# Padded pools with 64-byte shifts, a new order inside attention items, and bias tiles on the GpSimd queue in a two-layer diffusion backbone

## The chip, the cores and the metric

The kernel runs on one core of one Trainium2 chip. A core has TensorE (PE in the profile; its weight loads are PEld), VectorE (DVE), ScalarE (ACT), GpSimd (POOL) and SyncE (SP), one on-chip memory (SBUF) of 128 partitions, and matmul accumulators (PSUM). Transfers between main memory and SBUF are requested on the queues of SP, POOL and ACT. The metric is the device time of one execution in microseconds.

## The reference

The reference computes two layers over 1,024 latent tokens (`x`, on a grid of 16 rows by 64 columns) and 256 context tokens, each of width 1,024:

- layer 0: RMS norm and modulation, an input projection (1,024 to 2,048 columns), a 2-D Fourier transform over 512 of the channels beside an order-2 Hyena long convolution over the others, and an output projection; then a SwiGLU feed-forward network (FFN) with 2,816 hidden units, for latent and context tokens.
- layer 1: neighbourhood attention with 16 heads of 64, then output projection and FFN for the latent tokens alone, and a last RMS norm.

In the attention a latent query sees a window of local keys with a bias per relative position, and all context keys, in one softmax:

```python
s_loc = einsum(q_r, k_b) * scale + bias          # masked outside the window
s_ctx = einsum(q_r, kc) * scale
p = softmax(concatenate([s_loc, s_ctx], axis=-1), axis=-1)
o = einsum(p_loc, v_b) + einsum(p_ctx, vc)
```

## The kernel before

**Number format and matmuls.** Weights and activations of nearly all products are split in two fp32r parts, high and low (`split`, lines 278 to 282: ACT copies the high part, DVE subtracts to get the low one), and three matmuls (high·high, high·low, low·high) take the place of one. Each matmul loads its stationary operand anew. Widths of the moving operand are 512 for latent tokens (`pc` 0 and 1), 256 for context tokens (`pc` 2) and 384 for the local keys in attention.

**Pools.** SBUF is cut into tile pools in the order of their creation (lines 205 to 211): `cp` (constants), `p4` (20 tiles of 4 KB per partition), `p2` (35 of 2 KB), `pg` (4 of 2 KB), `pt` (6 of 2 KB and small ones), `pko` (4 of 2 KB, named `tk`), `pw` (two each of `wh`, `wl`, `ws`, 4 KB). Tiles of `p4` and `p2` are named `s` in the profile, of `pg` `g`, of `pt` `t`; `mat` and `cs` are other names for the slots of `pw`. In the built program every tile of `p4`, `p2`, `pg` and the 2 KB tiles of `pt` starts 96 bytes past a multiple of 128 bytes, and every tile of `pko` and `pw` 32 bytes past one.

**Who uses `pw`.** `weights` (line 292) loads 512 KB of a weight matrix into `ws` or an `s` tile and splits it to a pair from `pair2` (`wh` and `wl`) or, in the context FFN, `pair3` (every third pair from the two `ws` slots). The high and low parts are then stationary operands of `lin` (line 319), whose moving operands are `s` tiles: input projection (16 blocks of 128 columns, each 8 row blocks, 3 matmuls, widths 256, 512 and 512), output projection (8 blocks, widths 512 and 256, and then 512 alone), context FFN (22 blocks for gate and up, width 256), the key and query projections in `attn_prep`, and the second output projection. Queries and the second output projection read the moving operand through a strided view with runs of 16 numbers (64 bytes). In `values` the roles are turned: `wh` and `wl` are the moving operand. `cmat` (line 306) loads a Fourier matrix as fp16 into `ws` and ACT widens it to `mat`, which is stationary in the spectra (width 512) and moving in the inverse transform `hy_inverse` (width 256). The latent FFN is a Strassen-Winograd scheme with seven products (`wino_steps`, matmuls at line 1246); two of the seven take their weights from `wh` and `wl`, the others from `s` and `t` tiles. Its down projection (`down`, line 1413) has both operands in `s` tiles; the context's down projection (line 1516) takes weights from `wh` and `wl` at width 256.

**Order.** A scheduler orders the instructions of each engine from its own estimate of times; buffers that come free and the order in which the program text creates the work set the rest. Each engine and each queue works in order.

**Attention.** `attention` (line 1648) runs 64 items (head, half of the rows, pair of column groups) through three stages, one item ahead, and weaves in the projections of the next pair of heads (`attn_prep`), or at the end the first part of the output projection (`first_part`), as other work for PE. Stage 1 of `attn_item` (line 1674) requests two bias tiles (`g`, 192 KB each, on SP's queue, `pg` has four) and computes context scores of both groups into one PSUM tile and local scores into two. Stage 2: DVE takes the maximum of the context scores (L1699), adds the bias and takes the maximum for each group (L1701), negates both maxima in one instruction (L1703); ACT makes four exponentials in the order bias tile 0, context 0, bias tile 1, context 1 (L1706, L1707); DVE adds the sums and inverts them (L1709, L1710); PE transposes the context probabilities and then each group's local ones (L1715), ACT and DVE split them into two fp16 parts (L1718, L1719). Stage 3 multiplies by the values, 30 matmuls of 64 columns. On POOL's queue in this stretch are copies of the halves of the queries into the other 64 partitions (`s<-s`, line 1632), stores of the attention's output (`d<-tk`, from L1757 and L1758), and, near the end, pieces of the output projection's weights (`ws<-in_w_out`) and the residual stream.

Of the kernel before, what the change touches and what calls it, by code (L numbers as in the profile page):

```python
# [10 lines left out]
F32 = mybir.dt.float32  # L11
F32R = mybir.dt.float32r
F16 = mybir.dt.float16
AF = mybir.ActivationFunctionType
# [4 lines left out]
P = 128  # L19
# [11 lines left out]
KSTART = (0, 8, 24, 32)  # L31
BOPS = ("B11", "B21", "T2", "T1", "T3", "B22", "T4")
# [167 lines left out]
class Builder:  # L200
    def __init__(self, ctx, tc, a, out, taps=None, stop=None):
        self.tc, self.nc, self.a, self.out = tc, tc.nc, a, out
        self.taps, self.stop = taps, stop
        ent = ctx.enter_context
        self.cp = ent(tc.tile_pool(name="cp", bufs=1))
        self.p4 = ent(tc.tile_pool(name="p4", bufs=20))
        self.p2 = ent(tc.tile_pool(name="p2", bufs=35))
        self.pg = ent(tc.tile_pool(name="pg", bufs=4))
        self.pt = ent(tc.tile_pool(name="pt", bufs=6))
        self.pko = ent(tc.tile_pool(name="pk", bufs=4))  # L210
        self.pw = ent(tc.tile_pool(name="pw", bufs=2))
        self.pp = ent(tc.tile_pool(name="pp", bufs=6, space=bass.MemoryType.PSUM))
        self.pq = ent(tc.tile_pool(name="pq", bufs=2, space=bass.MemoryType.PSUM))
        self.dr = ent(tc.tile_pool(name="dr", bufs=1, space=bass.MemoryType.DRAM))
        self.k = self.mk = self.pk = 0
        self.banks = 8
        self.sq = {}

# [67 lines left out]

    def pair3(self):

        self.p3 = (getattr(self, "p3", 0) + 1) % 3
        return self.pair2(("ws", "ws") if self.p3 == 0 else ("wh", "wl"))  # L290

    def weights(self, src, w=1024, cut=False, keep=None, wide=False, load=None):
        st = self.S4() if wide else self.pw.tile([P, 1024], F32, tag="ws", name=self.nm("ws"))
        if keep:
            hi, lo = keep
        else:
            hi, lo = self.pair3() if wide == 3 else self.pair2()
        (load or self.ld)(st.rearrange("p (n k) -> p n k", n=4) if cut else st[:, :w], src)
        self.split(st[:, :w], hi[:, :w], lo[:, :w])
        return hi, lo  # L300
# [5 lines left out]
    def cmat(self, w, src, view=None, small=False):  # L306
# [8 lines left out]
        m = self.mat(w)  # L315
# [506 lines left out]
    def hy_inverse(self, sq, o, y):  # L822
# [8 lines left out]
        for h in range(H // hw):  # L831
# [25 lines left out]
            for part, fi, i, fb in mats:  # L857
                ms[(i, fb)] = self.cmat(min(nb, 2) * 512, a["vi_" + sq][h, i, :, fb:fb + min(nb, 2)],
                                        lambda t: t.rearrange("p (f c) -> p f c", c=512), False)
# [431 lines left out]
    def ffn(self, l, u, h, hs, second, after, keep=None, begun={}):  # L1291
# [21 lines left out]
        todo = iter(())  # L1313
        if u is not None:
            for fb in range(NFB):
                wide = 3 if fb < NFB - 2 else True
# [77 lines left out]
    def down(self, l, bops, sops, hidc, hs, h, todo, after, keep):  # L1394
# [98 lines left out]
        if l == 0:  # L1493
# [4 lines left out]
            for kb in range(NFB):  # L1498
# [9 lines left out]
                wh, wl = self.pair2()  # L1508
# [165 lines left out]
    def attn_item(self, head, hd, hf, c0, qs, kk, kc, vt, osb, out):  # L1674
# [5 lines left out]
        for i in (0, 1):  # L1680
            c = c0 + i
            b = self.G(F32, 384)
            self.ld(b, a["bias"][head, hf, c])
# [15 lines left out]
        nc.vector.tensor_reduce(cm, pctx.rearrange("p (i k) -> p i k", i=2), axis=AX, op=MAX)  # L1699
        for i in (0, 1):  # L1700
            nc.vector.tensor_tensor_reduce(bias[i], loc[i][:, :384], bias[i], 1.0, cm[:, i:i + 1], ADD, MAX,  # L1701
                                           mx[:, i:i + 1])
        nc.vector.tensor_scalar(nm, mx, -1.0, None, op0=MUL)  # L1703
        pc = self.T()
        for i in (0, 1):
            nc.scalar.activation(bias[i], bias[i], AF.Exp, bias=nm[:, i:i + 1], accum_out=s1[:, i:i + 1])  # L1706
            nc.scalar.activation(pc[:, i * 256:i * 256 + 256], pctx[:, i * 256:i * 256 + 256], AF.Exp,  # L1707
                                 bias=nm[:, i:i + 1], accum_out=s2[:, i:i + 1])
        nc.vector.tensor_tensor(s1, s1, s2, ADD)  # L1709
        nc.vector.reciprocal(rv, s1)  # L1710
        pts = []
        for src, n in ((pc, 4), (bias[0], 3), (bias[1], 3)):
# [7 lines left out]
            pts.append(t)  # L1720
# [437 lines left out]
```

## Time and profile before

| | |
|---|---|
| median of three runs | 3058.11 us (3051.83 to 3061.61) |
| the profiled execution | 3055.81 us, span 3054.0 us |
| granted TensorE clock, mean | 0.985 |
| matmuls | 16,320 |
| ACT busy, POOL busy (share of span) | 46%, 15% |
| moved by DMA | 549.87 MB, mean 180 GB/s |
| largest group of matmuls | L1246, `s` by `s`, 2,028 of 128x512 |

In the profile a row such as `ps<-s,wh` names the output tile, the moving operand and the stationary operand, with buffer numbers left out. Times are microseconds from the start of the span. A matmul's shown duration reaches into the next one's, since they are pipelined; the distance between starts is what one costs.

### The profile page before, as it was taken

How to read it: one execution, taken by the hardware profiler on the slowest of the kernel's cores; microseconds unless marked ns; L12 is line 12 of the kernel's file. 1: busy time of each engine (PE TensorE's matmuls, PEld its weight loads, DVE VectorE, ACT ScalarE, POOL GpSimd, SP SyncE). 2: the span in 40 equal slices, each digit the busy share in tenths (PEclk: the TensorE clock that was granted, in tenths of full speed). 3: DMA queues.
4: the chain of work that ended last, by engine and by line, in shares of the span. 5: the costliest groups of instructions: out<-in, count | busy, mean ns of one | idle time of the engine just before them, and what ended most of it. 6: DMA issues, size and time to landing. Idle time of an engine off the chain costs nothing. (4 is left out here: it accounts for less than half of the span.)

```text
span 3054.0 us, 45753 instructions
## 1 busy us (share of the span) xinstructions
PE 2919.6 (96%) x16320; PEld 2420.3 (79%) x16320; DVE 2076.6 (68%) x3924; ACT 1390.4 (46%) x2581; POOL 460.3 (15%) x751
## 2 busy tenths in 40 slices
PE   7899999999999999999999999999889999999997
PEld 2678888888899788787778888888777788887886
DVE  5767785775677777866677437777676977664545
ACT  4663225453454333333445336777675533333433
POOL 1012012451101111212010000110111022112000
PEclk9999999999999999999999999999999999999999
DMA  6564545466555454659874334454555266535663
GB/s 250 190 204 169 182 141 155 124 199 206 210 172 200 170 181 170 215 177 325 299 252 165 131 126 116 127 143 124 164 180 187 97 234 221 173 111 175 214 193 131
DMA packets 263486, 549.87 MB, mean 180 GB/s; under 512 B 33878, under 2 KB 85784, under 8 KB 263258
## 3 DMA queue, kind: packets, MB, share of 16 engines
q1 hardware_dynamic: 209658, 381.23, 38.5%
q0 software_dynamic: 51296, 161.52, 15.1%
q10 hardware_dynamic: 2304, 4.20, 0.4%
q8 instruction: 128, 2.10, 0.3%
q14 instruction: 100, 0.82, 0.1%
HBM read 418.63 MB, written 119.80 MB: 176 GB/s over the span
## 5 line engine op out<-in xcount | busy, mean ns | idle before, releaser
L1246 PE MATMUL ps<-s,s 128*128 128x512 f32 x2028 | 513.0, 395 | 14.3 <-ACT g L1251 11.0
L1246 PEld LDWEIGHTS ps<-s,s 128*128 128x128 f32 x2028 | 384.6, 190 | 103.4 <-ACT g L1251 13.4
L276 PE MATMUL ps<-s,wh 128*128 128x256 f32 (+1 forms) x1768 | 391.7, 327 | 1.3 <-ACT wh L280 1.3
L276 PEld LDWEIGHTS ps<-s,wh 128*128 128x128 f32 x1768 | 291.4, 188 | 37.2 <-ACT wh L280 3.4
L276 PE MATMUL pq<-s,wh 128*128 128x512 f32 (+1 forms) x984 | 300.9, 384 | 10.3 <-DVE s L1630 7.6
L280 ACT CAST wh<-ws 128x1024 fp32r<-128x1024 f32 (+1 forms) x139 | 142.6, 1026 | 351.2 <-PE ps L276 163.2
L1413 PE MATMUL ps<-s,s 128*128 128x512 f32 (+1 forms) x1000 | 258.6, 384 | 11.2 <-DVE s L282 11.0
L282 DVE TENSOR_TENSOR wl<-ws,wh 128x1024 fp32r<-128x1024 f32 (+1 forms) x139 | 165.7, 1192 | 142.2 <-ACT wh L280 137.3
L280 ACT CAST s<-s 128x1024 fp32r<-128x1024 f32 (+2 forms) x188 | 171.7, 942 | 197.9 <-DMA s<-d 160.1
L276 PE MATMUL ps<-s,wl 128*128 128x256 f32 (+1 forms) x884 | 255.1, 326 | 1.1 <-DVE wl L282 1.1
L276 PE MATMUL ps<-s,s 128*128 128x64 f16 (+3 forms) x2663 | 216.5, 233 | 16.2 <-DVE s L1719 5.9
L1413 PEld LDWEIGHTS ps<-s,s 128*128 128x128 f32 x1000 | 183.7, 188 | 53.0 <-DVE s L282 17.1
L282 DVE TENSOR_TENSOR s<-s,s 128x1024 fp32r<-128x1024 f32 (+2 forms) x166 | 190.7, 1184 | 45.4 <-ACT s L280 44.8
L280 ACT CAST s<-t 128x512 fp32r<-128x512 f32 (+2 forms) x250 | 140.4, 579 | 175.6 <-DVE t L1225 67.6
L276 PEld LDWEIGHTS pq<-s,wh 128*128 128x128 f32 x984 | 177.8, 190 | 45.9 <-DVE s L1630 9.9
L282 DVE TENSOR_TENSOR s<-t,s 128x512 fp32r<-128x512 f32 (+2 forms) x250 | 164.4, 671 | 58.6 <-ACT s L280 32.9
L1246 PE MATMUL ps<-s,wh 128*128 128x512 f32 x608 | 194.9, 398 | 2.0 <-DVE g L1337 2.0
L276 PE MATMUL ps<-s,mat 128*128 128x512 f32 x684 | 180.9, 410 | 6.2 <-ACT s L280 3.2
L276 PE MATMUL pq<-s,wl 128*128 128x512 f32 (+1 forms) x492 | 183.0, 381 | 0.0
L276 PEld LDWEIGHTS ps<-s,wl 128*128 128x128 f32 x884 | 162.1, 188 | 18.5 <-DVE wl L282 1.7
L316 ACT CAST mat<-cs 128x1024 fp32r<-128x1024 f16 (+2 forms) x120 | 111.7, 935 | 131.6 <-PE ps L276 52.4
L276 PEld LDWEIGHTS ps<-s,mat 128*128 128x128 f32 x684 | 132.0, 196 | 43.6 <-DVE s L282 5.4
(379 smaller groups left out, 5666.0 us busy)
## 6 DMA issues: line engine op xcount, KB each, us to landing
s<-d SPq DMA_DIRECT2D x286, 256.0 KB, 3.6
s<-in_down SPq DMA_DIRECT2D x154, 256.0 KB, 4.0
d<-s POOLq DMA_DIRECT2D x137, 256.0 KB, 3.6
d<-tk POOLq DMA_DIRECT2D x98, 256.0 KB, 3.7
s<-in_ada_w POOLq DMA_DIRECT2D x48, 512.0 KB, 4.7
g<-in_bias SPq DMA_DIRECT2D x128, 192.0 KB, 2.9
ws<-in_up SPq DMA_DIRECT2D x44, 512.0 KB, 3.5
d<-g POOLq DMA_DIRECT2D x87, 256.0 KB, 3.3
```

The lines of the kernel that those rows point to most:

```text
L276: self.nc.tensor.matmul(o, l, r, start=st, stop=sp)
L280: self.last_hi = nc.scalar.copy(hi, src).ins
L282: self.last_lo = eng.tensor_tensor(lo, src, hi.bitcast(F32), SUB).ins
L316: self.nc.scalar.copy(m, st)
L1246: nc.tensor.matmul(ps, x[:, sl], y, start=first and j == 0 and x is wh and y is xh, stop=j == 3 and x is wl, skip_group_check=True)
L1413: m = nc.tensor.matmul(acc[j][:, c0:c1], x[:, sl], y[:, xs], start=first and k == 0, stop=last and k == 2, skip_group_check=True)
```

## The change

Three things change.

1. **Addresses.** A pad of 288 bytes is put in front of the constants and one of 448 bytes into `pt`, each with a memset on POOL. The 4 KB tiles of `pw` that are "shifted" are allocated with 4,224 bytes and used from byte 64 on; since a slot takes the size of its largest tile, all slots of `pw` grow by 128 bytes. In the built program the tiles of `p4`, `p2`, `pg`, `pt` (2 KB) and `pko` then start at a multiple of 128 bytes, the unshifted tiles of `pw` too, and the shifted ones 64 bytes past one. Shifted are: all pairs of the context FFN (the third pair in the `ws` slots too, and the last two blocks), `mat` in `hy_inverse`, and the weights of the context's down projection. Modulo 256, the slots of `pw` stand alternately at 0 and 128.
2. **Order inside an item.** Each group's maximum is negated right after it is known, in an instruction of its own (128 in place of 64). ACT's order becomes context 0, bias tile 0, context 1, bias tile 1. PE's transposes begin with bias tile 0, then the context probabilities, then bias tile 1.
3. **Queue.** The 128 bias tiles are requested with `ldr` (POOL) in place of `ld` (SP).

The instructions up to the values' projection keep their order on PE, ACT and DVE; from there on the scheduler interleaves items and projections differently, with the same matmuls.

```diff
+PAD_C, PAD_T, SHIFT = 72, 112, 16
...
+        self.pad(self.cp, PAD_C)
...
+    def pad(self, pool, w):
+        self.nc.gpsimd.memset(pool.tile([P, w], F32, name="pad", tag="pad", bufs=1), 0.0)
...
+    def shifted(self, tag, name, w=1024):
+        return self.pw.tile([P, 1056], F32R, tag=tag, name=self.nm(name))[:, SHIFT:SHIFT + w]
+
+    def pair1(self):
+        return self.shifted("wh", "wh"), self.shifted("wl", "wl")
+
     def pair3(self):
         self.p3 = (getattr(self, "p3", 0) + 1) % 3
-        return self.pair2(("ws", "ws") if self.p3 == 0 else ("wh", "wl"))
+        tags = ("ws", "ws") if self.p3 == 0 else ("wh", "wl")
+        return [self.shifted(g, n) for g, n in zip(tags, ("wh", "wl"))]
...
-            hi, lo = self.pair3() if wide == 3 else self.pair2()
+            hi, lo = self.pair3() if wide == 3 else self.pair1() if wide == 2 else self.pair2()
...
-    def cmat(self, w, src, view=None, small=False):
+    def cmat(self, w, src, view=None, small=False, shift=False):
...
-        m = self.mat(w)
+        if shift:
+            self.mk ^= 1
+            m = self.shifted(("wh", "wl")[self.mk], "mat", w)
+        else:
+            m = self.mat(w)
...
                 ms[(i, fb)] = self.cmat(min(nb, 2) * 512, a["vi_" + sq][h, i, :, fb:fb + min(nb, 2)],
-                                        lambda t: t.rearrange("p (f c) -> p f c", c=512), False)
+                                        lambda t: t.rearrange("p (f c) -> p f c", c=512), False, True)
...
+        if l == 0:
+            self.pad(self.pt, PAD_T)
         if u is not None:
             for fb in range(NFB):
-                wide = 3 if fb < NFB - 2 else True
+                wide = 3 if fb < NFB - 2 else 2
...
-                wh, wl = self.pair2()
+                wh, wl = self.pair1()
                 self.ld(f.rearrange("p (r k) -> p r k", r=2), w[kb].rearrange("r p k -> p r k"))
...
-            self.ld(b, a["bias"][head, hf, c])
+            self.ldr(b, a["bias"][head, hf, c])
...
+        pc = self.T()
         for i in (0, 1):
             nc.vector.tensor_tensor_reduce(bias[i], loc[i][:, :384], bias[i], 1.0, cm[:, i:i + 1], ADD, MAX,
                                            mx[:, i:i + 1])
-        nc.vector.tensor_scalar(nm, mx, -1.0, None, op0=MUL)
-        pc = self.T()
-        for i in (0, 1):
-            nc.scalar.activation(bias[i], bias[i], AF.Exp, bias=nm[:, i:i + 1], accum_out=s1[:, i:i + 1])
+            nc.vector.tensor_scalar(nm[:, i:i + 1], mx[:, i:i + 1], -1.0, None, op0=MUL)
             nc.scalar.activation(pc[:, i * 256:i * 256 + 256], pctx[:, i * 256:i * 256 + 256], AF.Exp,
                                  bias=nm[:, i:i + 1], accum_out=s2[:, i:i + 1])
+            nc.scalar.activation(bias[i], bias[i], AF.Exp, bias=nm[:, i:i + 1], accum_out=s1[:, i:i + 1])
...
-        pts = []
-        for src, n in ((pc, 4), (bias[0], 3), (bias[1], 3)):
+        pts = [None] * 3
+        for k, src, n in ((1, bias[0], 3), (0, pc, 4), (2, bias[1], 3)):
...
-            pts.append(t)
+            pts[k] = t
```

## The prediction

> **What bounds the kernel now.** I read the page's busy shares first, then a table of four stretches, then the instructions in order of time on PE, then the waits inside the attention stretch.
>
> ```profile
> span 3054.0 us, 45753 instructions
> PE 2919.6 (96%) x16320; PEld 2420.3 (79%) x16320; DVE 2076.6 (68%) x3924; ACT 1390.4 (46%) x2581; POOL 460.3 (15%) x751
> ```
>
> The table of stretches (busy time of PE, PEld, DVE, ACT, POOL, then granted clock, DMA share and GB/s) cuts the span into everything before attention, attention, output projection, and the second layer's FFN:
>
> ```profile
> 0.00:1830.00 1830.00, 1760.64 (x9082) 1459.03 (x9083) 1248.50 (x2386) 766.54 (x1180) 304.73 (x462) 0.99 0.57 192
> 1830.00:2305.00 475.00, 440.09 (x4040) 376.26 (x4038) 342.06 (x846) 333.17 (x963) 59.58 (x113) 0.99 0.49 143
> 2305.00:2390.00 85.00, 81.00 (x387) 63.67 (x388) 62.76 (x91) 41.10 (x70) 14.96 (x28) 0.96 0.56 196
> 2390.00:3054.00 664.00, 637.85 (x2815) 521.30 (x2813) 423.30 (x602) 249.57 (x369) 81.05 (x149) 0.98 0.51 171
> ```
>
> PE is busy nearly everywhere at a clock near 1, so the time is the number of matmuls times their pace. The pace is the distance between starts, not the duration shown, since matmuls overlap. Here are runs of PE's timeline (start, length of the run, line, tiles, count); the distance from one start to the next row's start, over the count, is the pace:
>
> ```profile
> 400.40 0.74 PE L276 MATMUL ps<-s,wl 128*128 128x256 f32 x3
> 400.98 1.32 PE L276 MATMUL ps<-s,wh 128*128 128x256 f32 x6
> ```
> ```profile
> 613.96 5.84 PE L276 MATMUL ps<-s,mat 128*128 128x512 f32 x24
> 619.64 0.27 PE L776 MATMUL pq<-c,s 128*128 128x128 f32 x1
> ```
> ```profile
> 692.87 0.88 PE L276 MATMUL ps<-s,s 128*128 128x256 f32 x6
> 693.59 0.86 PE L276 MATMUL pq<-s,s 128*128 128x512 f32 x3
> ```
> ```profile
> 1065.15 5.63 PE L1246 MATMUL ps<-s,s 128*128 128x512 f32 x24
> 1070.62 0.40 PE L1246 MATMUL ps<-s,wh 128*128 128x512 f32 x1
> ...
> 1072.95 1.32 PE L1246 MATMUL ps<-s,s 128*128 128x512 f32 x5
> ```
> ```profile
> 2365.66 0.63 PE L276 MATMUL ps<-s,wh 128*128 128x512 f32 x2
> 2366.13 0.40 PE L276 MATMUL ps<-s,wl 128*128 128x512 f32 x1
> 2366.37 0.64 PE L276 MATMUL ps<-s,wh 128*128 128x512 f32 x2
> ```
>
> And two stretches that hold one kind of matmul alone (context FFN, 256 wide, stationary in wh/wl; `values`, 512 wide, moving wh/wl):
>
> ```profile
> 900.00:940.00 40.00, 40.00 (x355) 40.00 (x354) 28.47 (x35) 22.04 (x30) 3.78 (x7) 1.00 0.66 219
> 1710.00:1750.00 40.00, 40.00 (x176) 32.85 (x175) 18.83 (x31) 15.50 (x25) 0.00 (x0) 1.00 0.43 145
> ```
>
> The paces in ns. 512 wide with both operands in `s` tiles: (1070.62 - 1065.15)/24 = 227.9. Ten 512-wide ones with the stationary in wh/wl, in the same loop at once afterwards: (1072.95 - 1070.62)/10 = 233.0. Stationary `mat` (the same slots): (619.64 - 613.96)/24 = 236.7. 512 wide with a strided moving view and wh/wl: (2366.37 - 2365.66)/3 = 236.7. 256 wide with wh/wl: 40.00/355 = 112.7. 256 wide with both in `s`: (693.59 - 692.87)/6 = 120.0. A 256+512+512 group of the input projection (rows that merge widths): 580. `values`: 40.00/176 = 227.3.
>
> So the pace goes with the pools that the operands lie in, and the built program says what differs: `s` tiles start 96 bytes past a multiple of 128, wh/wl/ws/mat 32 bytes past. Stationary and moving operand are 0 bytes apart (mod 128) in the `s`,`s` rows and 64 apart in the others. At 512 columns 0 apart is faster by 5 to 9 ns; at 256 columns 64 apart is faster by 7.
>
> **The change part by part.** Everything is summed against the profiled execution, 3055.81 us, which is 2.3 us below the median of the three runs.
>
> *Addresses.* Two pads and a 4,224-byte tile put `s` tiles at multiples of 128 and unshifted weight tiles too (0 apart); shifted ones stand 64 on. What gets the shift is the context FFN, the inverse's `mat` tiles and the context's down projection, all 256 wide, so they stay 64 apart; what is left unshifted is mostly 512 wide and goes from 64 to 0. The pairs:
>
> ```profile
> L1246 PE MATMUL ps<-s,wh 128*128 128x512 f32 x608 | 194.9, 398 | 2.0 <-DVE g L1337 2.0
> L276 PE MATMUL ps<-s,mat 128*128 128x512 f32 x684 | 180.9, 410 | 6.2 <-ACT s L280 3.2 <-DVE s L282 3.0
> L1246 PE MATMUL ps<-s,wl 128*128 128x512 f32 x304 | 120.5, 397 | 0.0
> L276 PE MATMUL pq<-s,mat 128*128 128x512 f32 x132 | 39.7, 413 | 2.1 <-DVE s L282 2.0
> ```
>
> - FFN products A11/A12: 608 + 304, with 144 more in pq by the loops (11 blocks, 2 matrices, 2 layers, 24 each), 1,056 x (233.0 - 227.9) = -5.4 us.
> - Spectra with `mat`: 816 x (between 233.0 and 236.7, say 235, less 227.9) = -5.8. These stretches wait for operands as well (6.2 us in the row), so I count half: -2.9.
> - Input projection, 384 groups by its loops: 580 against 2 x 227.9 + 120.0 = 575.8, -1.6. Output projection: 192 pairs of 512+256 about even, 192 single 512s at -5.1 ns, -1.0.
> - Key projections in attention: 384 x -5.1 ns = -2.0, and 192 of 256 columns x (120.0 - 112.7) = +1.4.
> - Strided views (query projections, second output projection): 768 between 236.7 and 227.9. Their 64-byte runs also stop straddling a 64-byte line, which no row prices; I take half, -3.4.
> - `values` is at 227.3 already: 0.
> - The wide moves on ACT and DVE and the pad memsets: 0. The memsets are two POOL instructions, and POOL is idle 85% of the span.
>
> That is about -15 us. Its ends: in the built program half of the unshifted tiles lie 128 bytes off modulo 256, a case no row shows, so the gain may be nothing and the 256-wide ones with shifted weights may lose up to 6 ns on half of some 1,600 (+5, and +1 from the keys): +6. With the spectra and views in full it is -24.
>
> [...]
>
> *Order inside attention items.* The transposes used to begin with the context probabilities, which wait for the last of four exponentials; now group 0's bias tile goes first, after the second one.
>
> ```profile
> PE ps L1715 <- ACT t L1707: 8.6, 12, 1.3
> PE ps L276 <- DVE st L1701: 4.2, 8, 0.9
> PE ps L1715 <- DVE st L1701: 1.6, 2, 1.4
> ```
> ```profile
> L1703 DVE TENSOR_SCALAR st<-st x64: 149/169/226, 1843.8 to 2304.0; 128x2 f32<-128x2 f32 x64
> ```
> ```profile
> L1707 ACT ACTIVATE t<-ps,st x128: 450/467/511, 1844.7 to 2305.9; 128x256 f32<-128x256 f32 x128
> ```
>
> PE waits 8.6 us for the context exponentials (467 ns each). Late next is the bias exponential of group 1, now the last of the four, in front of the last three transposes alone. I take half: -4. The price is 64 more negations on DVE, 64 x 0.169 = 10.8 us; DVE is busy 342 of 475 us there, and what covers them is its idle 133 us. Where they stand in front of a subtraction that PE waits for they cost at most what the wait behind DVE can grow. Ends: -10 to +5.
>
> *Bias tiles on POOL's queue.* Requests wait for a `g` buffer, which item k's transposes free for item k+2. Today that wait stands on SP; behind it stand value tiles and weights. Now it stands on POOL, and behind it the query half copies (s<-s), the attention outputs and the late w_out2 pieces; and the bias stands behind those.
>
> ```profile
> SPq L261 <- PE ps L1715: 308.9, 71, 12.5
> ```
> ```profile
> DVE g L1701 <- DMA g<-in_bias: 10.2, 8, 3.5
> ```
> ```profile
> POOL s L267 <- ACT s L1629: 50.6, 7, 12.6
> POOL ws L267 <- DVE st L1703: 30.9, 3, 14.3
> ```
> ```profile
> g<-in_bias SPq DMA_DIRECT2D x124, 192.0 KB, 2.7
> s<-s POOLq DMA_DIRECT2D x60, 128.0 KB, 3.7
> ```
> ```profile
> L267 POOL DMA_DIRECT2D s<-s x60 | 31.2, 520 | 163.8 <-ACT s L1629 50.6 <-DVE st L1699 29.3 <-DVE s L1719 27.9
> ```
>
> A request costs POOL 0.52 us, 128 of them 67 us, beside 60 busy of 475. Landing is later by about 1.0 us (3.7 against 2.7). Eight items already wait for their bias. If 20 of 64 wait 1 us longer at DVE, 20 us, and PE feels a tenth of it as its waits behind L1701 are short (5.8 us over all items), that is +2. SP is relieved, but no row shows PE waiting for what it loads there. Ends: -3 (all that PE waits behind DVE's bias sums, halved) and +28 (below).
>
> Sum: -15 - 4 + 2 = -17, so 3055.8 - 17 = 3038.8; I say 3039.
>
> **The rivals.**
> - *The pace is not set by addresses* (0 apart helps only where both tiles share one pool): -4 and +2 for the attention parts leave 3053.8, and with the +6 of the address term's bad end 3059.8; say 3055. For it: no row has a 128-byte offset. Against it: the paces split cleanly by pool in four places of the program.
> - *More comes off*: spectra and views in full (-24), the attention waits nearly gone (-10), no loss on the queue: 3022. For it: PE sits at 96% and has cover for little else. Against: the operand waits of the spectra remain.
> - *POOL's order makes the bias late (slower).* An item takes 475/64 = 7.4 us. A query copy that waits 7.2 us (50.6/7) puts a bias behind it late by 7.2 + 0.5 + 3.7 - 7.4 = 4.0 us, seven times 28; a w_out2 piece that waits 10.3 makes 7.1, three times 21. That is 49 us at DVE. PE today waits 5.8 us behind L1701 against 10.2 of DVE's bias waits, so at most 0.57 of it, 28 us: 3055.8 - 15 - 4 + 28 = 3065; with the longest waits (12.6) seven times and a lost pace gain it passes 3080. It decides from about 33 us of lateness at DVE, where 0.57 of it eats the 19 us gained. Against it: POOL is busy an eighth of the stretch, and the bias is asked for an item ahead. [...]
>
> **How the numbers follow.** The forecast has 0.55 (its own range 3026 to 3048), more comes off 0.15, no pace effect 0.14, bias late 0.16. A measurement of this kernel can tell about 0.3%, 9 us, from no change. Against the median of 3058.1, below 3049 counts as faster: the first two, 0.70. No pace effect is same, 0.14; a late bias is slower in nearly all of its span, 0.16. The range 3014 to 3066 takes in the ends of the pace term (-24 to +6) with a moderate lateness.
>
> **What would show it.** In the changed profile, FFN rows with wh/wl beside s,s rows should both step by about 228 ns, `mat` runs by 228 to 230, and strided views below 234; context FFN should stay at 113. PE's span before attention should shrink by some 10 us, which is pace alone, since the order of work there is unchanged. In attention, waits of L1715 for the context exponential should be halved, and DVE's waits for g<-in_bias stay under 30 us. The prediction is wrong if wh/wl rows remain at 233, or if bias waits pass 33 us.

## The result and the profile after

The changed kernel takes 3047.43 us (median of 20 runs, 3040.91 to 3057.43); the kernel before took 3058.36 us beside it (20 runs, 3049.44 to 3069.22). The ratio is 0.9967, with a 95% interval of 0.9956 to 0.9978: 10 us less, 7 to 13 by the interval. The profiled execution took 3048.99 us. It became faster, as forecast, by a little over half of the 19 us forecast against the median.

The page of the changed kernel, span and engines, and two of the four stretches shown of the kernel before (busy time of PE, PEld, DVE, ACT, POOL, granted clock, DMA share, GB/s):

```profile
span 3047.2 us, 45763 instructions
PE 2906.5 (95%) x16320; PEld 2420.2 (79%) x16320; DVE 2076.2 (68%) x3988; ACT 1392.6 (46%) x2581; POOL 530.7 (17%) x881
```
```profile
0.00:1830.00 1830.00, 1752.84 (x9076) 1458.23 (x9077) 1245.95 (x2385) 765.54 (x1180) 306.88 (x466) 0.99 0.57 192
1830.00:2305.00 475.00, 443.92 (x4087) 381.42 (x4087) 348.14 (x919) 339.72 (x975) 128.26 (x240) 0.99 0.49 148
```

POOL's busy time in attention rose from 59.58 to 128.26 us, 68.7 us for the bias requests, which were put at 67. PE's work per matmul fell, but not as foreseen. Here is the FFN of layer 0 in PE's timeline (start, length, tiles, count), one block with weights in one slot of a pair and one block with weights in the other:

```profile
1068.94 0.39 PE L1264 MATMUL ps<-s,wh 128*128 128x512 f32 x1
...
1071.21 2.88 PE L1264 MATMUL ps<-s,s 128*128 128x512 f32 x12
...
1085.72 0.64 PE L1264 MATMUL ps<-s,wh 128*128 128x512 f32 x2
...
1088.28 0.39 PE L1264 MATMUL ps<-s,wl 128*128 128x512 f32 x1
```

Ten matmuls lie between the first two rows: 2.27 us, 227 ns each. Eleven lie between the last two: 2.56 us, 232.7 ns each, as slow as before (233.0). In the built program the first slot stands 0 bytes from the moving operand modulo 256, the second 128. The two stretches of one kind alone (context FFN and `values`) read:

```profile
900.00:940.00 40.00, 40.00 (x356) 40.00 (x355) 29.23 (x36) 22.29 (x32) 3.78 (x7) 1.00 0.64 217
1710.00:1750.00 40.00, 40.00 (x175) 32.67 (x175) 18.93 (x32) 15.15 (x26) 0.00 (x0) 1.00 0.43 145
```

From start to start the context FFN stays at 113.3 ns, as expected; `values` went from 228.9 to 230.3, one half of its tiles having become slower. (The counts in such a row take in a matmul or two that only reach into the stretch. Dividing by them, as the prediction did for its 112.7 and 227.3, gives a pace that is 1 to 2 ns too low.)

In attention the waits of PE and DVE (what waits, for what: sum, times, longest):

```profile
PE ps L282 <- DVE st L1722: 7.9, 10, 1.5
PE ps L1734 <- DVE s L1738: 7.2, 11, 1.0
...
PE ps L1734 <- ACT g L1727: 0.8, 3, 0.5
```
```profile
DVE g L1722 <- DMA g<-in_bias: 5.1, 8, 1.7
```
```profile
g<-in_bias POOLq DMA_DIRECT2D x128, 192.0 KB, 3.1
```

and on the page of the kernel before:

```profile
g<-in_bias SPq DMA_DIRECT2D x128, 192.0 KB, 2.9
```

The 8.6 us that the transposes waited for the context exponential are gone. In their place PE waits for DVE: the value products for the bias sum (L1722, 7.9 against 4.2 us) and the transposes for the subtraction of the halves (L1738, 7.2). DVE's own waits for bias tiles halved, from 10.2 to 5.1 us; the experiments below show that this comes with the order and not with the queue. The tiles land 3.1 us after the request (median) where it was 2.9.

### The profile page after: what moved, and what is told of

It reads as the page before. It is cut to its first block, busy times and chain, and to the rows that moved or that the text cites. A ratio compares the mean times of both kernels' runs of the same rounds, so it can differ in the third digit from the quotient of the medians.

```text
span 3047.2 us, 45763 instructions
## 1 busy us (share of the span) xinstructions
PE 2906.5 (95%) x16320; PEld 2420.2 (79%) x16320; DVE 2076.2 (68%) x3988; ACT 1392.6 (46%) x2581; POOL 530.7 (17%) x881
## 5 line engine op out<-in xcount | busy, mean ns | idle before, releaser
L1264 PE MATMUL ps<-s,s 128*128 128x512 f32 x2028 | 511.2, 394 | 21.3 <-ACT g L1269 15.1
```

Of the source, the lines that this page charges most:

```text
L1264: nc.tensor.matmul(ps, x[:, sl], y, start=first and j == 0 and x is wh and y is xh, stop=j == 3 and x is wl, skip_group_check=True)
```

## The experiments

Times are compared as the ratio to the kernel before, run beside each on the same chip; what a ratio lacks to 1, times 3056, gives the us. Where paces are summed, a step is the time from one matmul's start to the next one's; there is one profile of each kernel, and a sum has a play of some tenths of a us by where the line between a pace and a stall is drawn.

**The three parts, each alone.** The addresses alone:

```diff
+PAD_C, PAD_T, SHIFT = 72, 112, 16
...
+        self.pad(self.cp, PAD_C)
...
+            self.pad(self.pt, PAD_T)
...
+        return self.pw.tile([P, 1056], F32R, tag=tag, name=self.nm(name))[:, SHIFT:SHIFT + w]
```

> The pads and shifts alone; attention as before, and the order of all instructions too. Theory A (the pace goes with the distance of the two operands modulo 256, and the change brings only half of the unshifted tiles to distance 0, the other half to 128): FFN rows with wh/wl alternate between about 227 and 233 ns, the strided views get slower (240 in place of 237 at distance 128), and the sum is small: about -3 us, ratio 0.999, between -6 and 0. Theory B (addresses give the whole gain, the attention parts nothing): -11 us, ratio 0.9965.

Measured: 0.9967 (0.9954 to 0.9981), 10.1 us less. Here PE, DVE and ACT run the same instructions in the same order as before (POOL has the two memsets more), so the two profiles can be subtracted matmul by matmul (start to next start, in all 16,320). Steps where neither profile shows a stall are pace: -7.6 us; the rest, stalls, -5.4 us in this one execution. The rows are those of theory A, alternating by slot, but its sum of -3 us was too small, and the time is the one that theory B names. By kinds: FFN products with wh/wl -3.6, the other FFN matmuls -1.8, the 512-wide keys -1.9, `mat` at 512 columns -1.5, the output projections -1.5, and losses of 0.3 to 0.8 each in the queries, `values`, the input projection, the context FFN and the 256-wide keys.

The order inside attention items alone:

```diff
-        nc.vector.tensor_scalar(nm, mx, -1.0, None, op0=MUL)
...
-            nc.scalar.activation(bias[i], bias[i], AF.Exp, bias=nm[:, i:i + 1], accum_out=s1[:, i:i + 1])
+            nc.vector.tensor_scalar(nm[:, i:i + 1], mx[:, i:i + 1], -1.0, None, op0=MUL)
...
+            nc.scalar.activation(bias[i], bias[i], AF.Exp, bias=nm[:, i:i + 1], accum_out=s1[:, i:i + 1])
...
-        for src, n in ((pc, 4), (bias[0], 3), (bias[1], 3)):
+        for k, src, n in ((1, bias[0], 3), (0, pc, 4), (2, bias[1], 3)):
```

> The new order inside attention items alone, addresses and queue as before. Theory A (attention gave most of the gain, by the order): -6 us, ratio 0.998, all of it between the first and the last item, with the wait of the transposes for the context exponential (8.6 us) gone. Theory B (addresses give the gain): 0 within 2 us. A third one (the queue gives the attention's gain): 0 here too, and the gain in the queue's run.

Measured: 0.9975 (0.9963 to 0.9987), 7.6 us less, which is theory A; PE's wait for the context exponential is gone. DVE's waits for bias tiles, still requested on SP here, are 6.4 us in place of 10.2.

The bias tiles on POOL's queue alone:

```diff
-            self.ld(b, a["bias"][head, hf, c])
+            self.ldr(b, a["bias"][head, hf, c])
```

> The bias tiles on the GpSimd queue alone. Theory A: within 2 us of before, DVE's waits for bias tiles between 5 and 15 us. The third theory (the queue gives the attention's gain, by taking 309 us of blocked time from SP): -6 us. The rival of the prediction (late bias tiles): slower by 10 us or more, with DVE waiting over 30 us for bias.

Measured: 1.0016 (1.0002 to 1.0029), 4.9 us more: a small loss, and none of the three forecasts for the time, though DVE's waits are those of theory A. The rows of this run's attention stretch, to be held against the ones of before (PE behind the bias sum 4.2, DVE for bias 10.2 with at most 3.5 us at once, SP behind the transposes 308.9 us):

```profile
PE ps L276 <- DVE st L1701: 7.3, 9, 2.2
```
```profile
DVE g L1701 <- DMA g<-in_bias: 9.9, 9, 4.2
```
```profile
SPq L261 <- PE ps L1715: 84.8, 13, 13.6
```
```profile
POOL g L267 <- PE ps L1715: 143.1, 32, 11.3
```

The wait for a free buffer moved from SP to POOL as described. DVE's bias waits did not grow in sum (9.9 against 10.2 us), but the longest did (4.2 against 3.5). PE's wait behind the bias sum grew by 3.1 us, and its wait for the sum with the residual stream near the end of the stage (L1990) from 1.4 to 3.8 us. The attention stage, by landmarks, is 5.3 us longer; 3.4 us of that is slow clock (below). That the later bias tiles cause these waits is not shown. The three parts sum to -12.8 us; together they give -10.

**The address distance.** Next, with order and queue as before, the tiles were moved so that no unshifted weight tile stands 128 off, with a shift of 192 bytes for those that want one:

```diff
-PAD_C, PAD_T, SHIFT = 72, 112, 16
+PAD_C, PAD_T, SHIFT = 8, 48, 48
...
-        return self.pw.tile([P, 1056], F32R, tag=tag, name=self.nm(name))[:, SHIFT:SHIFT + w]
+        return self.pw.tile([P, 1072 if tag == "ws" else 1088], F32R, tag=tag, name=self.nm(name))[:, SHIFT:SHIFT + w]
```

> As the first run, but with the slots of wh and wl 4,352 bytes apart, so that every unshifted weight tile is at distance 0 modulo 256, and the shift 192 bytes. Theory A (period 256): FFN rows with wh/wl all near 227 ns, strided views near 233, the inverse's matmuls 115 in place of 117.5; by the counts FFN -6.6, spectra -2, views -3, keys -1, inverse -2: about -14 us, ratio 0.9955. If the period is 128 or the addresses do not matter: the same as the first run.

Measured: 0.9977 (0.9965 to 0.9989), 7.0 us less, where -14 was expected, and no better than the first layout. All FFN rows were at 227 ns, 6.8 us off their sum, but the context FFN went from 113.3 to 118.4 ns and lost 4.7 us, and the context's down projection 1.5. To learn the rule by itself, the pace was measured alone:

```diff
+    for form in "fhuv":
+        for m in (0, 8):
+            for d in range(0, 128, 8) if form in "fh" else range(0, 128, 16):
+                group(form + "ab"[m // 8] + "abcdefghijklmnop"[d // 8], form, m, d)
```

> This kernel leaves the whole computation out (its output is zeros) and runs PE alone: groups of 48 matmuls, 128x128 stationary, moving 512 wide, 256 wide or 512 wide through a strided view, nothing to wait for; from group to group only the distance of the stationary's address from the moving operand's changes, by 32 bytes from 0 to 480, with the moving operand at a multiple of 256 and at 32 bytes past one. Its time is no verdict on anything; read are the starts of the matmuls. Theory A, the pace depends on the distance modulo 256 alone: 512 wide some 227 ns at 0 and 256 and 233 at 64, 128, 192 and again at 320, 384, 448; 256 wide some 114 at 64, 192, 320 and 448 and 119 at 0, 128, 256, 384; the same for both places of the moving operand. Theory B, the period is 512: 512 wide 227 at 0 only, with 256 as slow as 128; 256 wide 192 unlike 448, which would be why the context FFN went from 114 to 118 at a distance of 192 in the run with tiles at multiples of 256. Theory C, the distance is not what counts, and the paces in the program come from what other engines read and write at the same time: here, with the other engines idle, all distances of one width run within 1 ns of each other.

Its timeline (the third letter of the tile is the distance, a is 0 bytes, b is 32 and so on; f is 512 wide, h is 256 wide):

```profile
53.04 11.05 PE L61 MATMUL faa<-x,w 128*128 128x512 f32 x48
63.92 11.35 PE L61 MATMUL fab<-x,w 128*128 128x512 f32 x48
75.12 11.36 PE L61 MATMUL fac<-x,w 128*128 128x512 f32 x48
86.32 11.40 PE L61 MATMUL fad<-x,w 128*128 128x512 f32 x48
97.55 11.32 PE L61 MATMUL fae<-x,w 128*128 128x512 f32 x48
108.71 11.37 PE L61 MATMUL faf<-x,w 128*128 128x512 f32 x48
119.91 11.16 PE L61 MATMUL fag<-x,w 128*128 128x512 f32 x48
130.91 11.36 PE L61 MATMUL fah<-x,w 128*128 128x512 f32 x48
142.10 11.05 PE L61 MATMUL fai<-x,w 128*128 128x512 f32 x48
152.99 11.35 PE L61 MATMUL faj<-x,w 128*128 128x512 f32 x48
...
409.35 5.92 PE L61 MATMUL haa<-x,w 128*128 128x256 f32 x48
415.10 5.84 PE L61 MATMUL hab<-x,w 128*128 128x256 f32 x48
420.78 5.82 PE L61 MATMUL hac<-x,w 128*128 128x256 f32 x48
426.43 5.79 PE L61 MATMUL had<-x,w 128*128 128x256 f32 x48
```

Start to next start over 48: at 512 columns 226.7 ns at a distance of 0, then 233.3, 233.3, 234.0 (96 bytes), 232.5 (128), 233.3, 229.2 (192), 233.1, and 226.9 again at 256. So the period is 256 bytes and only 0 gets the full gain; 192 gets most of it, which fits `values`, at 192 before the change and at 226 to 230 then. Moving both operands by 32 bytes together changes nothing (226.8 to 227.4 at 0, 233.4 at 64). The other engines are idle here, so nothing that they read or write makes these 7 ns: theory C falls, and so does theory B's period of 512. Theory A holds at 512 columns, but for the 192. At 256 columns it does not: 0 is the slowest, with 160 beside it (119.8), 64 gives 117.7 and nothing is below 117.4, while the same 64 bytes ran at 113.3 ns in the context FFN. What gives those last 4 ns is not settled; the run of all-zero addresses with the exponentials, below, shows that it is not the distance.

The strided views do not follow the plain rule either. In the queries' view a distance of 0 gives 239.3 ns, 64 gives 237.5 and 128 gives 241.4, so against the 64 of before the queries can only lose; in the second output projection's view 0 gives 231.6 against 236.5 at 64. With both operands 32 bytes on, where its runs of 64 bytes cross a boundary of 64, a view at a distance of 0 runs within 0.3 ns of the same.

Then the address part once more with all 512-wide pairs at 0 and the 256-wide ones at 64 or 192: slots of 4,352 bytes, no second pad, and the shift given to the other group of tiles, so that the layout fits:

```diff
-PAD_C, PAD_T, SHIFT = 72, 112, 16
+PAD_C, SHIFT = 72, 48
...
-            self.pad(self.pt, PAD_T)
...
-        return [self.pw.tile([P, 1024], F32R, tag=g, name=self.nm(n)) for g, n in zip(tags, ("wh", "wl"))]
+        return [self.shifted(g, n) for g, n in zip(tags, ("wh", "wl"))]
...
+    def plain(self, tag, name, w=1024):
+        n = 1056 if tag == "ws" else 1088
+        return self.pw.tile([P, n], F32R, tag=tag, name=self.nm(name))[:, :w]
```

> The address part alone, order as before, with every 512-wide pair at a distance of 0 modulo 256 (weight slots of 4,352 bytes, so that none stands 128 off) and the 256-wide ones of the context FFN, the inverse and the context's down projection at 64 or 192. From the paces of the isolated matmuls and of the runs so far: FFN products 1,056 x (233.3 - 226.8) = -6.9 us instead of half of it, spectra 816 x some -5 = -4, strided views -1.5, the keys about -1, the rest of the 512-wide ones some -3 as in the run with tiles at multiples of 256, and no loss in the 256-wide ones: some -17 us of pace. Theory A, the prediction's sum for the addresses (-15) was right for tiles that stand at 0 and too large only because half of them stand 128 off: -14 to -20 us, some 3039 us, ratio 0.994, all FFN rows at 227. Theory B, what PE gains in pace beyond the first 8 us comes back as waits for operands, since ACT, DVE and the transfers set the rest: the pace in the trace is as above but the time stays at -10 us, ratio 0.9967, like the changed kernel's own addresses alone.

Measured: 0.9949 (0.9932 to 0.9965), 15.6 us less (11 to 21). Its FFN with wh/wl, ten matmuls from the first row to the second, is at 227.0 ns; the context FFN, in the stretch of one kind, at 118.2 from start to start:

```profile
1072.80 0.39 PE L1268 MATMUL ps<-s,wh 128*128 128x512 f32 x1
...
1075.07 2.88 PE L1268 MATMUL ps<-s,s 128*128 128x512 f32 x12
```
```profile
900.00:940.00 40.00, 40.00 (x340) 40.00 (x340) 28.63 (x35) 21.96 (x31) 3.78 (x7) 1.00 0.61 209
```

Matmul by matmul the pace is 11.0 us better than before: FFN with wh/wl -6.8, other FFN -2.1, `mat` -3.6, keys and queries at 512 columns -1.4, `values` -1.0, against +4.3 in the context FFN, which had not been expected. Of the two theories the one by which pace turns back into waits (0.9967) is just outside the interval; the other is inside. Its advantage over the changed kernel's own addresses, 5.5 us, lies within what the two intervals leave open.

**Parts together.** Addresses and order, with the bias tiles back on SP:

```diff
-            self.ldr(b, a["bias"][head, hf, c])
+            self.ld(b, a["bias"][head, hf, c])
```

> The changed kernel with its bias tiles requested on SP again, as before: addresses and order without the queue. Theory A, the three parts add, as their single runs say (-10.1, -7.6 and +4.9 us against -10.9 for all): -17.7 us, some 3040.5 us, ratio 0.994, and faster than the changed kernel by 5 to 7 us. Theory B, the queue costs something only with the old order of the transposes, since it is group 0's bias that PE now takes first and the POOL queue brings it no later: the same as the changed kernel, -11 us, ratio 0.9965. In the trace, by A the SP queue's waits behind the transposes are above 300 us in attention again, and PE's waits in attention are no longer than in the run of the order alone.

Measured: 0.995 (0.9933 to 0.9968), 15.3 us less; some 5 us less than the changed kernel, as when the queue was tried alone. The two intervals overlap, but twice the queue cost 5 us, and never gained. As theory A has it, SP's waits behind the transposes are back (310.5 us) and PE's waits in the stage are no longer than with the order alone (33.8 and 34.6 us). DVE waits 5.7 us for bias tiles here, on SP, and 5.1 us in the changed kernel, on POOL: with this order the queue does not bring them late, and the halving against before is the order's. The all-zero addresses (the diff above) with the order (the diff of the order alone):

> The addresses of the run before it in this call with the new order inside attention items and the bias tiles on SP. Theory A, the parts add: -17 - 7.6 = some -24 us, 3032 us, ratio 0.992, faster than the changed kernel by some 13 us. Theory B, more pace turns into waits: no faster than addresses and order with half of the tiles 128 off, ratio 0.995.

Measured: 0.994 (0.9924 to 0.9956), 18 us less. The sum of the parts (-23) lies at the edge of the interval; the value is nearer to the case where more pace brings no more (0.995).

**The order, taken apart.** The exponentials, with the negation for each group, but without the transposes, against the kernel with the order alone:

```diff
-        for k, src, n in ((1, bias[0], 3), (0, pc, 4), (2, bias[1], 3)):
+        for k, src, n in ((0, pc, 4), (1, bias[0], 3), (2, bias[1], 3)):
```

> Of the order inside items only the first half: the negation for each group and the context exponential ahead of the bias one; the transposes begin with the context probabilities as before, addresses and queue as before. Theory A, it is the order of the transposes that gains, since PE then needs only the second exponential done to start and not the third: this half -1 to -3 us, and PE still waits some 5 us for the context exponential. Theory B, the exponentials' order does it, the context exponential of group 1 being the third of four now, 0.61 us earlier in each of 64 items: -6 to -8 us.

And the transposes without the exponentials, against the kernel before:

```diff
-        pts = []
-        for src, n in ((pc, 4), (bias[0], 3), (bias[1], 3)):
+        pts = [None] * 3
+        for k, src, n in ((1, bias[0], 3), (0, pc, 4), (2, bias[1], 3)):
...
-            pts.append(t)
+            pts[k] = t
```

> Of the order inside items only the second half: group 0's bias tile is transposed first, the exponentials stand in the old order, in which it is the first of the four; one negation for both groups as before. Theory A: -5 to -8 us, nearly all of the -7.6, and PE's wait for the context exponential is gone. Theory B: -1 to -2 us, since the context probabilities that come second still wait for the last of the four exponentials and PE's wait only moves behind the first three transposes (0.33 us).

Measured: the exponentials alone 0.9942 (0.9926 to 0.9958), 17.7 us less; the transposes alone 1.0014 (0.9998 to 1.003), 4 us more, which their interval does not tell from nothing. The theory by which the transposes' order gains fell: it gains nothing, and beside the exponentials it takes 10 us away again (7.6 against 17.7, and these two intervals do not touch). PE's waits in the attention stretch, in the run of the exponentials alone:

```profile
PE ps L1714 <- DVE st L1702: 8.2, 9, 1.8
PE pq L276 <- DVE s L1630: 4.7, 7, 1.9
PE ps L276 <- DVE st L1702: 3.6, 8, 0.6
```

and of the transposes alone:

```profile
PE ps L276 <- DVE st L1701: 12.2, 14, 3.1
PE ps L1715 <- DVE st L1701: 4.2, 5, 1.2
PE ps L276 <- ACT t L1707: 3.7, 4, 1.7
```

and of both together:

```profile
PE ps L276 <- DVE st L1702: 13.2, 13, 2.7
PE ps L1714 <- DVE s L1718: 4.5, 8, 0.6
```

With group 0's bias tile first, the value products (line 276, ps) wait 12 to 13 us for DVE's bias sum; with the context first 4 us, in both pairs of runs. Part of that only moves, since the transposes (L1714, L1715) wait for the same sum too: all of PE's waits for it are 5.8 us before and 16.4 with the transposes alone, 11.8 with the exponentials alone and 16.3 with both. In the changed kernel the same step back is the other way about (11.0 with the transposes' order, 13.5 without, below), so this place is likely where the order costs, but not shown to be. DVE's bias sum in its turn waits for PE's local scores, longer with both than with the exponentials alone:

```profile
DVE g L1702 <- PE ps L276: 36.0, 17, 3.0
```
```profile
DVE g L1702 <- PE ps L276: 18.9, 10, 2.5
```

That difference is in all the kernels with the new exponentials: 35 to 36 us with the transposes' order, 17 to 21 without. Why PE makes the scores later there is not shown.

**A stall costs more than its length.** The 17.7 us are more than the 8.6 us of waiting that could go, and the granted clock has part of the rest. First PE's longest wait in attention before, then three consecutive stretches of that kernel around it, then the whole of attention and the second output projection for before, the exponentials alone and the transposes alone (PEclk is the first of the last three columns):

```profile
PE pq L276 <- DVE s L1630: 7.6, 7, 4.6
```
```profile
2220.39:2223.80 3.41, 0.00 (x0) 0.00 (x0) 1.43 (x4) 0.33 (x1) 1.04 (x2) 1.00 1.08 364
2223.80:2230.63 6.83, 5.93 (x14) 4.67 (x15) 2.43 (x11) 4.42 (x16) 0.52 (x1) 0.50 0.38 78
2230.63:2237.46 6.83, 6.42 (x93) 5.91 (x93) 4.93 (x11) 4.83 (x11) 0.56 (x1) 1.00 0.43 126
```
```profile
1815.00:2370.00 555.00, 516.00 (x4416) 436.26 (x4415) 395.52 (x925) 369.31 (x1027) 72.50 (x136) 0.99 0.50 149
```
```profile
1815.00:2370.00 555.00, 526.32 (x4492) 447.92 (x4491) 413.45 (x1010) 381.85 (x1041) 76.82 (x144) 1.00 0.51 156
```
```profile
1815.00:2370.00 555.00, 512.87 (x4390) 435.09 (x4389) 391.76 (x918) 367.98 (x1021) 72.73 (x136) 0.98 0.49 146
```

PE stood for all of the first stretch, in a wait of 4.6 us for L1630; then its clock was granted at 0.50 for 6.83 us, and a 512-wide matmul took twice its time. Another such stretch, in the FFN of layer 1 of the kernel before, shows it:

```profile
2410.84 2.50 PE L1246 MATMUL pq<-s,s 128*128 128x512 f32 x5 [0.22 <-DVE s L1147]
2413.14 2.05 PE L1246 MATMUL ps<-s,s 128*128 128x512 f32 x4
```

2.30 us for five, 460 ns each against 227. Between 1815 and 2370 us the kernel before has three such stretches, of 6.83, 3.41 and 3.41 us, the run of the exponentials one of 3.41. The table takes the stage from the same first to the same last matmul in each profile; waits are the sum of the rows of PE's waits, the loss is half of the time at 0.50, in us:

| kernel | stage | waits | clock loss | change of both | change of stage |
|---|---|---|---|---|---|
| before | 555.0 | 38.1 | 6.8 | | |
| changed | 549.2 | 34.1 | 6.8 | -4.0 | -5.8 |
| queue alone | 560.3 | 41.0 | 10.2 | +6.3 | +5.3 |
| order alone | 547.2 | 34.6 | 3.4 | -6.9 | -7.8 |
| exponentials alone | 537.1 | 28.1 | 1.7 | -15.1 | -17.9 |
| transposes alone | 561.1 | 41.1 | 10.2 | +6.4 | +6.1 |

What is left over is under 3 us in each row. So the waits and the slow clock behind the longest of them carry the stage. (The stage is not the whole: in the profile of the exponentials alone what follows it took 5.3 us more than before, 6.3 us of slow clock more among it.) In the 71 slow stretches between 1700 and 3030 us of the thirteen whole kernels' profiles PE had been busy for 0 to 2.3 of the 3.41 us before. Of 58 single gaps of 2 us and more there, 53 had slow clock in them or in the 3.41 us behind, of 35 gaps of 1.5 to 2 us nine; and in the changed kernel a stretch at 1855 us came with no gap before it longer than 0.73 us.

**Two last kernels.** Both take this edit, the first in the kernel of all-zero addresses and order, the second in the changed kernel:

```diff
-        for k, src, n in ((1, bias[0], 3), (0, pc, 4), (2, bias[1], 3)):
+        for k, src, n in ((0, pc, 4), (1, bias[0], 3), (2, bias[1], 3)):
```

> Addresses with every 512-wide pair at a distance of 0 modulo 256, the exponentials' new order with the old order of the transposes, and the bias tiles on SP. Theory A, the two gains add (-15.6 and -17.7 as ratios of their own runs): -33 us, some 3023 us, ratio 0.989, faster than every run so far. Theory B, both feed on the same slack of ACT and DVE in attention, where the address run also shortened the stage by 5 us: -22 to -26 us, ratio 0.992.

Measured: 0.9914 (0.9899 to 0.9929), 3030.74 us, 26 us less (22 to 31): the fastest of all, though its interval meets those of the all-zero addresses with the order and of the exponentials alone. This is theory B; the full sum of 33 lies outside. Its attention stage is 533.2 us, with 26.5 us of waits. But not all of its lead over the all-zero addresses with the order (8 us) is the attention's. The context FFN, in the stretch of one kind:

```profile
900.00:940.00 40.00, 40.00 (x355) 40.00 (x355) 28.86 (x35) 22.34 (x32) 3.79 (x7) 1.00 0.65 220
```

From start to start this is 113.3 ns, where the all-zero addresses alone (340 matmuls in the same 40 us) and with the order had 118.2. In the built programs of the three every matmul before the attention stands at the same addresses, in the same order. So the last 4 to 5 ns at 256 columns are not set by the distance, nor by the layout. In these three profiles the pace changes from one value to the other behind an interruption of PE, and then stays: the same matmul follows a pause of 0.3 us at 852 to 854 us, and from there some 385 to 415 matmuls in a row run at one value or the other. What chooses between them is open. Between this profile and that of the all-zero addresses with the order it is 4.2 us over the context FFN, and no kernel's timed runs can be cleared of it, since only one execution of each was profiled.

The changed kernel with the edit:

> The changed kernel with one line undone: the transposes begin with the context probabilities again. Addresses, exponentials and POOL queue as changed. Theory A, the transposes' order costs in the changed kernel what it cost beside the exponentials alone (-7.6 with it, -17.7 without it): 10 us less than the changed kernel, some -21 us against before, ratio 0.993. Theory B, with the POOL queue the order of the transposes hardly matters, since the queue's wait for a freed bias buffer changes with it: the ratio stays at 0.9967 within 0.001, and the 10 us would be an accident of one program's schedule.

Measured: 0.995 (0.9937 to 0.9964), 15 us less, 5 us better than the changed kernel. That lies between the two theories and the intervals touch; the direction is that of the other runs, the size is open. Its profile lost 11.9 us to the slow clock in the stage, more than any other. DVE's bias waits are 14.7 us here, on POOL, against 10.4 with the exponentials alone on SP: with this order the queue may bring some tiles later.

## Why the prediction was right or wrong

The sign held, the likeliest case held, and the size was 8 us off. By its own terms:

- *Addresses, -15: measured -10.1, of which some -8 is pace.* The mechanism is right at 512 columns but for the period, and mis-sized. The step that failed is the price 227.9 for every tile left unshifted. The text had named half of the unshifted tiles as 128 off, "a case no row shows", and put a loss at the end of the range, but took the full gain. That case is worth nothing (232.5 ns alone, 232.7 in the FFN). FFN with wh/wl: -3.6 for -5.4; `mat`: -1.5 for -2.9; input projection +0.6 for -1.6; strided views -0.5 for -3.4, a gain of 0.8 in the output projection and a loss of 0.3 in the queries. The keys came nearly as written (-1.9 for -2.0, +0.8 for +1.4), the output projection too (-0.7 for -1.0). The other FFN matmuls had been left out, -1.8, and in that execution 5.4 us of stalls went, 3.4 of them slow clock; that part is luck of one execution as far as is known. The runs that "stop straddling" are worth nothing (0.3 ns at most, alone). With all tiles at 0 the term is -15.6 as timed and -11.0 in pace, near to what was written, but made up otherwise, with 4.3 us lost in the context FFN that no distance explains. So at 512 columns it was the layout that was read wrongly and not the price.
- *The price at 256 columns.* The 7 ns between 112.7 and 120.0 were put down to the distance. Alone, 64 bytes are worth 2 ns against 0 (117.7 and 119.8), and the rest comes and goes at the same addresses (113.3 and 118.2). That the context FFN stayed at 113 was expected for this reason and held, but the reason does not carry it.
- *The end of -24.* The addresses' terms with spectra and views in full make -21. No run of the addresses alone came near it (-15.6 at most).
- *`values` at 0*: half of its tiles came to 128 and lost 4.2 ns, the other half gained 1.4, +0.6 us in all. It had stood at a distance of 192, one of the two good ones (229.2 ns alone).
- *Order, -4: measured -7.6*, within the ends. The reason was half wrong: the gain was put down to the transposes starting with group 0's bias tile. The exponentials' order gains (-17.7), the transposes' order gives 10 of it back. "What is late next" was named as the bias exponential of group 1, which shows 0.8 us; it is DVE's bias sum and subtraction, 15.1 us in the two rows of after. The price of a wait was taken at its length, without the slow clock behind it.
- *Queue, +2: measured +4.9*, within -3 and +28. Requests cost POOL what was worked out (0.54 us each); landing is later by 0.2 us, not 1.0, a figure that set copies of 128 KB within the chip against loads of 192 KB; DVE's bias waits did not pass 33 us or come near, so the rival of late bias tiles failed. PE's waits in the stage grew by 2.9 us where DVE's for the bias did not grow (9.9 against 10.2), so neither the tenth nor the fraction of 0.57 describes what happened.
- *What would show it.* wh/wl at 228: half of the rows. Context FFN at 113: yes. The context exponential's wait halved: gone. Strided views below 234: the second output projection's at 0 alone, the queries' not. Bias waits under 30: 5.1. Before attention 10 us less: from PE's first matmul on 8.6 less in the address run alone and 9.3 in the one with addresses and order, but 1.3 more in the changed kernel's own profile and 1.0 less in that of the changed kernel with the old transposes, with the same work up to there. Between the changed kernel's profile and that of addresses and order it is 7.8 us more waits and 5.1 us more slow clock, so one profile cannot settle this sign.
- *The rival by which the pace is not set by addresses*, 3055: the isolated matmuls disagree, at 226.7 to 234.0 ns by distance alone with all other engines idle, and so does the FFN, where the slot at a distance of 0, in another pool than the `s` tiles, went from 233.0 to 227 ns.

So 5 us less from the addresses, 4 more from the order, 3 lost on the queue and 3 that the parts lose together make 10 for 17. That the size came out no further off is in part luck: the order gained more than its reason gave, by the half that the reason had not named. Each of these differences is about as large as its own interval; the half of the tiles at 128 alone is shown row by row in the trace.

## What to carry to other kernels

Before a layout is priced, list the address distance modulo 256 (here 226.7 ns at 0 and 233.3 at 64, with 512 columns) of every pair of operands in the built program, each buffer of a rotating pool by itself, and give a case that no row shows its own small measurement. Take a bundle of reorderings apart: here one half gave 17.7 us and the other took 10 of it back. Price a PE wait of 2 us or more at its length plus half of the slow-clock time that came in or behind 53 of 58 such waits here (1.7 us for a stretch of 3.41). And before a pace is put down to an address, see whether the same program runs at another pace at the same addresses: at 256 columns this one did.

## What the runs showed of the hardware

- Alone, with the other engines idle, 512-column matmuls step by 226.7 to 227.4 ns where stationary and moving address are equal modulo 256, 229.2 at 192, 232.5 to 234.0 at the other steps of 32 bytes. At 256 columns 0 and 160 are the worst, 119.8 against 117.4 to 118.5 in the other places. In the program the same 256-column matmuls, at the same addresses, ran at 113.3 ns in one profile and at 118.2 in two others; that is open.
- Slow-clock stretches are a good part of what differs between two profiles of the same work: 5.1 of the 10.6 us between the changed kernel's profile and that of addresses and order, from PE's first matmul to the attention. In the profile of before they cost up to 39 us, counted as half of their time (78.5 us), the stretch at the end of the kernel left out.
- 128 requests of 192 KB moved from SP's to POOL's queue cost 0.54 us of POOL each and some 5 us of the kernel's time (0.6 to 8.9 alone), though the tiles land only 0.2 us later and DVE does not wait longer for them in sum (9.9 against 10.2 us alone, 5.1 against 5.7 with addresses and order; 14.7 against 10.4 in the one other pair, which also differs in its addresses).
